# Conditioning weights of a decoder step's first norm, consumed in nine visits instead of one at a time, with seven more slots for weight chunks

## The chip, the cores and the metric

The kernel runs on one core of a Trainium2 chip. The metric is the device time of one execution in microseconds; lower is better. The core's engines work side by side, each in the order of its own instruction stream: TensorE (PE in the profile, with weight loads apart as PEld), VectorE (DVE), ScalarE (ACT), GpSimd (POOL) and SyncE (SP), which here issues the transfers of the weights. Matmuls read SBUF and write PSUM; DVE and ACT empty PSUM.

## The reference

One layer of a hybrid decoder for 256 prompt tokens and 8 x 4 sample tokens, 288 columns in all, model width 2048, in fp32:

```
mod = silu(c) @ w_ada + b_ada            # c: 1 prompt row + 8 sample rows; 6 parts of 2048
sh1, sc1, g1, sh2, sc2, g2 = split(mod, 6)
h = rmsnorm(x, norm1) * (1 + sc1) + sh1
proj = h @ w_in                          # u_pool 512 | z 1536 | xbc 2560 | dt 24
pool_out = pool_mixer(u_pool)            # trailing windows 2, 4, 8, 16
ssd_out = ssd_mixer(z, xbc, dt)          # conv, chunked scan, gated rmsnorm
x = x + g1 * (concat(pool_out, ssd_out) @ w_out)
h2 = rmsnorm(x, norm2) * (1 + sc2) + sh2
x = x + g2 * conv_ffn(h2)                # w_up, causal conv, silu gate, w_down
y = rmsnorm(x, norm_f)
```

The states (pool, conv, ssm, ffn) are outputs too.

## The kernel before

Activations lie with features on the partitions, 16 tiles of 128 features by 288 tokens. Each projection is made of three matmuls in a reduced fp32 format: weights and activations are split into a high and a low part, and `mm3` (L233 to L235) adds high x high, high x low and low x high. Splitting a weight chunk takes one ACT copy (L227) and one DVE subtraction (L228) in `split`.

All weights come as one stream of chunks of up to 128 x 1024 fp32 (512 KB), fetched by `load` on SP's queue into slots. The class `_W` holds the slots, eight for raw chunks (tag `raw`) and two for split ones (tag `wsp`); it goes round them in turn, so a load waits until the chunk in its slot has been used up.

The start of the layer is done in feature groups, `KGROUPS`: (0, 1), (1, 1), (2, 2), (4, 4), (8, 4), (12, 4), first tile and number of tiles. For each group two things are done. First, the shift and scale of its features are computed from `w_ada` ("conditioning", `ada_group_units`): 4, 4, 8, 16, 16, 16 chunks; each chunk's matmuls have the 32 columns of `sc_c` as their stationary operand, so four of them stand side by side in the array (`tile_position`), unsplit fp32, and all add up in one PSUM bank (`adag`). Then ACT copies the result (`asb_g`, L267), PE transposes it (`adat_g`, L273 or L309), DVE adds the bias, and `modulate` (L357 to L369) makes the group's operands `h1k`, high and low. Second, `xbc_units` multiplies the group's tiles with their part of `w_in` for 28 output tiles, called units; a unit has 3, 3, 6, 12, 12, 12 matmuls by group. After each unit its PSUM bank is emptied: copied by ACT in the first group, added by DVE in the later ones (L562) to `cvp`, `upp`, `ups` or `zy`.

The conditioning of the next group is interleaved with the units of the present one:

```
if i >= NX[gi]:
    next(nxt, None)          # one more chunk: matmuls of the last one, load of the next
if i == ET - 4:
    drain(nxt)
    modulate(...)            # operands of the next group
```

The last group has no such work; its loop first makes the dt projection (`mm_dt`) and `dt_stage`, then interleaves the Mamba part and later conditioning (`ada_part_units`, L331). That one already works in visits: four chunks are loaded, and their matmuls run in one piece, the chunk that was loaded last first, the others with high priority and kept in program order.

The program is written with a tile framework. It puts each engine's instructions in order by a model of when they can run, with program order as the priority, and adds the semaphores. A pool is a stretch of SBUF; pool `mx` holds the tiles of the first part of the layer. A tile with a tag shares the tag's slots with others of that tag: the input tiles `xa` and later the recurrent states (`h0`) are `blk`, four slots; the initial conv and pool states (`st`, loaded in `late_loads`, at the fifth group) and later the conv outputs are `cf`.

Of the kernel before, what the change touches and what calls it, by code (L numbers as in the profile page):

```python
# [11 lines left out]
F32 = mybir.dt.float32  # L12
# [5 lines left out]
P = 128  # L18
# [9 lines left out]
NH = 24  # L28
# [10 lines left out]
RAW1, RAW2 = 8, 1  # L39
SPLIT1, SPLIT2 = 2, 2  # L40
PHASE = (192, 32, 0)
YK = 2
NX = (10, 1, 1, 1, 1)
# [89 lines left out]
def kernel(ctx: ExitStack, tc, ins, outs):  # L133
# [148 lines left out]
    def ada_group_units(gi):  # L282

        k0, gk = KGROUPS[gi]
        nj = min(2 * gk, 4)
        nb = 2 * gk * P // nj
        per = RAWC // (nj * nb)
        ps = pa.tile([P, 512], F32, tag="ada", name=f"adag{gi}")
        for q in range(KT // per):
            raw = load(("ada", gi, q))  # L290
            yield
            if gk == 1:

                for kk in range(0, per, 2):
                    k = q * per + kk
                    for j in range(4):
                        nc.tensor.matmul(ps[32 * j:32 * j + 32, :nb], sc_c[:, k + j // 2, :],
                                         raw[:, kk * 256 + j * P:kk * 256 + j * P + P],
                                         start=(k == 0), stop=(k == KT - 2), tile_position=(0, 32 * j))
                if gi == 0 and q < WU[3]:  # L300
                    warm_pe(WU[2], raw[:, 0:P])
                continue
            for kk in range(per):
                ada_mm(ps, raw, q * per + kk, kk * nj * nb, nb, range(nj))
# [67 lines left out]
    class _W:  # L372
# [23 lines left out]
    mx = mx_ctx.enter_context(tc.tile_pool(name="mx", bufs=1))  # L396
    xa = []
# [45 lines left out]
    def late_loads():  # L443
# [3 lines left out]
        st = mx.tile([P, XT * NB * 3 + 4 * NB * 15], F32, tag="cf", name="st", bufs=2)  # L447
# [14 lines left out]
    def dt_stage(ps):  # L462
        tmp = kp.tile([NH, 4, N], F32, tag="hmod", name="dttmp", bufs=2)
        e, z, w, xb = (tmp[:, i, :] for i in range(4))
        t = mx.tile([NH, 2, N], F32, tag="cf", name="dtt", bufs=2)
# [16 lines left out]
        an = mx.tile([NH, 1], F32, name="an")  # L482
# [10 lines left out]
        tok = mx.tile([P, 2, 3, NH], F32, name="tok")  # L493
# [14 lines left out]
        csd = mx.tile([P, 2, 3, NH], F32, name="csd")  # L508
# [9 lines left out]
        ex = mx.tile([P, 2, NH], F32, name="ex")  # L518
# [5 lines left out]
        dm = mx.tile([32, NB, NH], F32, tag="cm", name="dm")  # L524
# [46 lines left out]
    def conv_group(g):  # L571
        cf = mx.tile([P, 5, CW], F32, tag="cf", name=f"cf{g}", bufs=2)
# [14 lines left out]
        ncv = mx.tile([P, 5, 27], F32, tag="ncv", name=f"ncv{g}")  # L587
# [32 lines left out]
    def ssd_group(g):  # L620
# [19 lines left out]
        bt = mx.tile([P, 3, P], F32, tag="bt", name=f"bt{g}")  # L640
# [10 lines left out]
        cb = mx.tile([P, N], F32, tag="cb", name=f"cb{g}")  # L651
# [7 lines left out]
        s1 = mx.tile([P, G6], F32, tag="s1", name=f"s1_{g}")  # L659
# [3 lines left out]
        hf = mx.tile([P, G6], F32, tag="hf", name=f"hf{g}")  # L663
# [5 lines left out]
        s2 = mx.tile([P, G6], F32, tag="s2", name=f"s2_{g}")  # L669
# [4 lines left out]
        cm = mx.tile([P, NB * 36], F32, tag="cm", name=f"cm{g}")  # L674
# [9 lines left out]
        yo = mx.tile([P, G6], F32, tag="yo", name=f"yo{g}")  # L684
# [7 lines left out]
        def decays(t):  # L692

            e = mx.tile([P, 2, N], F32, tag="e", name=f"e{g}_{t}", bufs=2)
            ec = mx.tile([P, 2, P], F32, tag="ec", name=f"ec{g}_{t}", bufs=2)
# [67 lines left out]
    def pool_units(g):  # L763
# [3 lines left out]
        for st in range(g + 1):  # L767
            tp = kp.tile([P, 15 + NP], F32, tag="xsq", name=f"pp{g}_{st}", bufs=2)
            ts_ = mx.tile([P, NB, 19], F32, tag="pools", name=f"pq{g}_{st}", bufs=2)
# [48 lines left out]
    drain(ada_group_units(0))  # L818
    modulate(xav(0, KGROUPS[0][1]), rstd1p, 0, 0, 0, KGROUPS[0][1], "g0")
# [452 lines left out]
```

## Time and profile before

| | us |
|---|---|
| median of 3 runs (lowest, highest) | 1378.83 (1378.32, 1379.18) |
| the profiled execution, its time | 1381.55 |
| the profiled execution, its span | 1379.8 |
| matmul xbc, L233, 448 of them, busy | 139.6 |
| matmul adag, L262, 512 records, busy | 39.9 |
| matmul adap, L331, 288 records up to 420 us, busy | 35.8 |

In a row of the profile, L262 is line 262 of the kernel, `x8` the number of instruction records taken together (a plain fp32 matmul leaves two), and a name such as `adag<-raw_ada,sc_c` says which tile is written from which. Starts and durations are in us from the start of the span. A bracket at the end of a row gives the engine's idle time ahead of it and what ended it. Matmuls are pipelined and their ends modelled, so the distance between starts says more than the duration.

### The profile page before, as it was taken

How to read it: one execution, taken by the hardware profiler on the slowest of the kernel's cores; microseconds unless marked ns; L12 is line 12 of the kernel's file. 1: busy time of each engine (PE TensorE's matmuls, PEld its weight loads, DVE VectorE, ACT ScalarE, POOL GpSimd, SP SyncE). 2: the span in 40 equal slices, each digit the busy share in tenths (PEclk: the TensorE clock that was granted, in tenths of full speed). 3: DMA queues.
4: the chain of work that ended last, by engine and by line, in shares of the span. 5: the costliest groups of instructions: out<-in, count | busy, mean ns of one | idle time of the engine just before them, and what ended most of it. 6: DMA issues, size and time to landing. Idle time of an engine off the chain costs nothing.

```text
span 1379.8 us, 26352 instructions
## 1 busy us (share of the span) xinstructions
PE 1358.6 (98%) x10565; PEld 1246.1 (90%) x10565; DVE 823.6 (60%) x1448; ACT 575.2 (42%) x925; POOL 232.0 (17%) x428
## 2 busy tenths in 40 slices
PE   9999999999999999999999999999999999999997
PEld 7677888777769998999999999999999999999997
DVE  3775657878774347745565445665654556566543
ACT  5222333378754334533443333434433334443452
POOL 0000001122122123211221001221120012132221
PEclk9999999999999999999999999999999999999998
DMA  8889887888878986688655555655555565555531
GB/s 340 308 297 310 306 289 259 303 304 296 329 283 318 354 289 249 215 295 293 209 185 181 172 173 183 200 190 189 179 182 173 177 194 189 196 191 196 183 119 69
DMA packets 97194, 323.20 MB, mean 234 GB/s; under 512 B 10736, under 2 KB 19888, under 8 KB 97072
## 3 DMA queue, kind: packets, MB, share of 16 engines
q1 hardware_dynamic: 93168, 310.63, 65.6%
q0 software_dynamic: 3184, 9.69, 1.9%
q8 instruction: 83, 1.36, 0.4%
q10 hardware_dynamic: 720, 1.19, 0.2%
q14 instruction: 39, 0.32, 0.1%
HBM read 309.78 MB, written 10.39 MB: 232 GB/s over the span
## 4 chain that ended last, share of the span: by engine, by line
PE 93%; DVE 3%; DMA 1%; ACT 1%; issue 1%; POOL 0%; SPq 0%; DVEq 0%; POOLq 0%; ACTq 0%
PE mm_down L234 7%; PE mm_down L235 7%; PE mm_down L233 7%; PE mm_val L234 6%; PE mm_gate L234 6%; PE mm_gate L233 6%; PE mm_val L235 6%; PE mm_gate L235 6%; PE mm_val L233 6%; PE xbc L233 5%; PE xbc L234 4%; PE xbc L235 4%; PE adap L331 4%; PE mm_out L234 3%; PE mm_out L233 3%; PE mm_out L235 2%
## 5 line engine op out<-in xcount | busy, mean ns | idle before, releaser
L234 PE MATMUL mm_down<-ahl,wsp_down 128*128 128x288 f32 x688 | 204.3, 297 | 0.0
L235 PE MATMUL mm_down<-ahl,wsp_down 128*128 128x288 f32 x688 | 202.8, 295 | 0.0
L233 PE MATMUL mm_down<-ahl,wsp_down 128*128 128x288 f32 x688 | 202.1, 294 | 0.0
L234 PE MATMUL mm_val<-h2k,wsp_val 128*128 128x288 f32 x640 | 190.1, 297 | 0.0
L234 PE MATMUL mm_gate<-h2k,wsp_gate 128*128 128x288 f32 x640 | 190.0, 297 | 0.0
L235 PE MATMUL mm_val<-h2k,wsp_val 128*128 128x288 f32 x640 | 188.8, 295 | 0.0
L235 PE MATMUL mm_gate<-h2k,wsp_gate 128*128 128x288 f32 x640 | 188.8, 295 | 0.0
L233 PE MATMUL mm_gate<-h2k,wsp_gate 128*128 128x288 f32 x640 | 188.8, 295 | 0.0
L233 PE MATMUL mm_val<-h2k,wsp_val 128*128 128x288 f32 x640 | 188.0, 294 | 0.0
L228 DVE TENSOR_TENSOR wsp_gate<-raw_gate,wsp_gate 128x1024 fp32r<-128x1024 f32 x80 | 98.0, 1226 | 137.6 <-ACT wsp_gate L227 137.6
L228 DVE TENSOR_TENSOR wsp_down<-raw_down,wsp_down 128x1024 fp32r<-128x1024 f32 x96 | 107.3, 1118 | 121.9 <-ACT wsp_down L227 121.0
L227 ACT CAST wsp_down<-raw_down 128x1024 fp32r<-128x1024 f32 x96 | 92.2, 960 | 167.3 <-PE mm_down L235 116.8
L227 ACT CAST wsp_gate<-raw_gate 128x1024 fp32r<-128x1024 f32 x80 | 83.9, 1050 | 162.2 <-PE mm_gate L235 71.3
L233 PE MATMUL xbc<-h1k,wsp_xbc 128*128 128x288 f32 x448 | 139.6, 313 | 3.5 <-ACT h1k L368 1.7
L227 ACT CAST wsp_val<-raw_val 128x1024 fp32r<-128x1024 f32 x80 | 84.1, 1051 | 119.7 <-issue 98.8
L234 PE MATMUL xbc<-h1k,wsp_xbc 128*128 128x288 f32 x448 | 133.4, 298 | 0.3 <-DVE h1k L369 0.3
L235 PE MATMUL xbc<-h1k,wsp_xbc 128*128 128x288 f32 x448 | 132.6, 298 | 0.1
L233 PEld LDWEIGHTS mm_down<-ahl,wsp_down 128*128 128x128 f32 x688 | 129.6, 188 | 0.0
L234 PEld LDWEIGHTS mm_down<-ahl,wsp_down 128*128 128x128 f32 x688 | 129.3, 188 | 0.0
L235 PEld LDWEIGHTS mm_down<-ahl,wsp_down 128*128 128x128 f32 x688 | 129.2, 188 | 0.0
L233 PEld LDWEIGHTS mm_gate<-h2k,wsp_gate 128*128 128x128 f32 x640 | 120.5, 188 | 5.0 <-ACT ahl L1037 4.2
L233 PEld LDWEIGHTS mm_val<-h2k,wsp_val 128*128 128x128 f32 x640 | 120.6, 188 | 0.0
(318 smaller groups left out, 3013.0 us busy)
## 6 DMA issues: line engine op xcount, KB each, us to landing
raw_adap<-wflat SPq DMA_DIRECT2D x128, 512.0 KB, 5.4
raw_gate<-wflat SPq DMA_DIRECT2D x80, 512.0 KB, 3.5
raw_val<-wflat SPq DMA_DIRECT2D x80, 512.0 KB, 3.6
raw_ada<-wflat SPq DMA_DIRECT2D x64, 512.0 KB, 5.7
raw_xbc<-wflat SPq DMA_DIRECT2D x55, 512.0 KB, 6.0
raw_down<-wflat SPq DMA_DIRECT2D x48, 512.0 KB, 3.6
raw_out<-wflat SPq DMA_DIRECT2D x32, 512.0 KB, 7.4
raw_down<-wflat SPq DMA_DIRECT2D x32, 384.0 KB, 3.0
```

The source lines that it names most:

```text
L227: nc.scalar.copy(hi[:, :n], raw[:, a:a + n])
L228: nc.vector.tensor_tensor(lo[:, :n], raw[:, a:a + n], hi[:, :n].bitcast(F32), ALU.subtract)
L233: nc.tensor.matmul(ps, whi[:, w], bh, start=first, stop=False)
L234: nc.tensor.matmul(ps, whi[:, w], bl, start=False, stop=False)
L235: nc.tensor.matmul(ps, wlo[:, w], bh, start=False, stop=last)
L331: i = nc.tensor.matmul(ps[32 * j:32 * j + 32, :512], sc_c[:, k, :], raw[:, (j % 2) * 512:(j % 2) * 512 + 512], start=(k == ay - 1), stop=( ...
```

## The change

Three things are done.

The conditioning of the groups after the first is consumed in visits. A visit loads four chunks (for the second and third group) or eight (for the fourth to sixth) and then runs their matmuls without a break, in the manner of the later conditioning. `VISIT` gives the size and the units after which a visit stands: after unit 10 of the first group's loop; 7 and 15 of the second's; 8 and 19 of the third's to fifth's. `MOD` gives how many units before the end `modulate` stands: 4, 5, 6, 6, 6.

Seven more raw slots (pool `w0`) are in use from the end of the first group's conditioning until the last group begins. They lie where tiles lie that are needed only from then on: those tiles move from pool `mx` to a pool `m2`, opened when `w0` is closed. `remove` takes the seven slots out of the round.

The tile `st` takes a `blk` slot instead of a `cf` slot.

```diff
+RAW0 = 7
-NX = (10, 1, 1, 1, 1)
+VISIT = {1: (4, (10,)), 2: (4, (7, 15)), 3: (8, (8, 19)), 4: (8, (8, 19)), 5: (8, (8, 19))}
+MOD = (4, 5, 6, 6, 6)
...
-        for q in range(KT // per):
-            raw = load(("ada", gi, q))
-            yield
...
+        n = 0
+        visit = VISIT[gi][0] if gi else 1
+        for v in range(0, nq, visit):
+            raws = [(q, load(("ada", gi, q))) for q in range(v, v + visit)]
+            if not gi:
+                yield
+            begun = False
+            for q, raw in raws[::-1]:
+                for j, k, w in steps(q, raw):
+                    with tc.high_priority() if begun else nullcontext():
+                        i = nc.tensor.matmul(ps[32 * j:32 * j + 32, :nb], sc_c[:, k, :], w, start=n < 4,
+                                             stop=n >= (KT if gk > 1 else KT // 2) * 4 - 4,
+                                             tile_position=(0, 32 * j))
+                    if begun:
+                        tc.keep_in_program_order(i)
+                    begun = gi > 0
+                    n += 1
                 if gi == 0 and q < WU[3]:
                     warm_pe(WU[2], raw[:, 0:P])
...
+            if gi:
+                yield
...
+        def remove(self, pool):
+            for tag, s in self.slots.items():
+                r = self.i[tag] % len(s)
+                self.slots[tag] = [x for x in s[r:] + s[:r] if x[0] is not pool]
+                self.i[tag] = 0
...
-        st = mx.tile([P, XT * NB * 3 + 4 * NB * 15], F32, tag="cf", name="st", bufs=2)
+        st = mx.tile([P, XT * NB * 3 + 4 * NB * 15], F32, tag="blk", name="st", bufs=4)
...
-        t = mx.tile([NH, 2, N], F32, tag="cf", name="dtt", bufs=2)
+        t = m2[0].tile([NH, 2, N], F32, tag="cf", name="dtt", bufs=2)
...
     drain(ada_group_units(0))
+    w0 = w0_ctx.enter_context(tc.tile_pool(name="w0", bufs=1, reuse_waits="tile"))
+    wp[0].add(w0, RAW0, 0)
...
         if last:
+            wp[0].remove(w0)
+            w0_ctx.close()
+            m2[0] = mx_ctx.enter_context(tc.tile_pool(name="m2", bufs=1, reuse_waits="tile"))
...
-                if i >= NX[gi]:
-                    next(nxt, None)
-                if i == ET - 4:
+                if i in VISIT[gi + 1][1]:
+                    next(nxt)
+                if i == ET - MOD[gi]:
                     drain(nxt)
                     modulate(xav(k0, gk), rstd1, 0, 0, k0, gk, f"g{gi + 1}")
```

More of the change, by code (lines that the diff above doesn't have):

```diff
@@ L288, in ada_group_units, with steps @@
         ps = pa.tile([P, 512], F32, tag="ada", name=f"adag{gi}")
-        for q in range(KT // per):
-            raw = load(("ada", gi, q))
-            yield
+        nq = KT // per
+        def steps(q, raw):
             if gk == 1:
                 for kk in range(0, per, 2):
-                    k = q * per + kk
                     for j in range(4):
-                        nc.tensor.matmul(ps[32 * j:32 * j + 32, :nb], sc_c[:, k + j // 2, :],
-                                         raw[:, kk * 256 + j * P:kk * 256 + j * P + P],
-                                         start=(k == 0), stop=(k == KT - 2), tile_position=(0, 32 * j))
+                        yield j, q * per + kk + j // 2, raw[:, kk * 256 + j * P:kk * 256 + j * P + P]
+            else:
+                for kk in range(per):
+                    for j in range(nj):
+                        c = (kk * nj + j) * nb
+                        yield j, q * per + kk, raw[:, c:c + nb]
+        n = 0
[15 more added lines that the diff above has]
+                    n += 1
                 if gi == 0 and q < WU[3]:
                     warm_pe(WU[2], raw[:, 0:P])
-                continue
-            for kk in range(per):
-                ada_mm(ps, raw, q * per + kk, kk * nj * nb, nb, range(nj))
+            if gi:
+                yield
         r = 32 * nj
@@ L396 @@
     mx = mx_ctx.enter_context(tc.tile_pool(name="mx", bufs=1))
+    m2 = [None]
+    w0_ctx = ExitStack()
     xa = []
```

34 lines of the change are left out of this document (17 added, 17 removed).

## The prediction

> **What bounds the kernel now.** I read the page first: span, engine shares, the chain that ended last.
>
> ```profile
> span 1379.8 us, 26352 instructions
> PE 1358.6 (98%) x10565; PEld 1246.1 (90%) x10565; DVE 823.6 (60%) x1448; ACT 575.2 (42%) x925; POOL 232.0 (17%) x428
> PE 93%; DVE 3%; DMA 1%; ACT 1%; issue 1%; POOL 0%; SPq 0%; DVEq 0%; POOLq 0%; ACTq 0%
> ```
>
> PE carries 93% of the chain, so a change pays if it takes time out of PE's own sequence, as long as nothing else becomes late. The change touches only the five feature groups before the last. I located each group in PE's timeline by counting xbc matmuls (28 units, three matmuls for each of 1, 1, 2, 4, 4 feature tiles: 84, 84, 168, 336, 336) and asked the table of windows for these stretches. The last row ends where the dt projection begins. Columns: stretch, length, busy PE, PEld, DVE, ACT, POOL, granted clock, DMA share, GB/s.
>
> ```profile
> 21.80:38.40 16.60, 16.48 (x166) 13.80 (x167) 7.92 (x13) 14.31 (x55) 0.65 (x2) 1.00 0.85 317
> 38.40:64.80 26.40, 24.65 (x239) 16.22 (x237) 17.54 (x58) 5.97 (x10) 1.46 (x2) 1.00 0.86 297
> 64.80:100.20 35.40, 34.59 (x282) 25.92 (x282) 25.98 (x72) 9.37 (x13) 1.69 (x2) 1.00 0.83 305
> 100.20:154.90 54.70, 54.70 (x446) 47.08 (x444) 34.98 (x77) 15.24 (x18) 2.85 (x7) 1.00 0.87 298
> 154.90:212.00 57.10, 57.10 (x470) 47.70 (x469) 32.75 (x75) 15.75 (x19) 0.99 (x2) 1.00 0.88 300
> ```
>
> PE is full in each row, DMA is 83 to 88% busy, and only ACT in the first group and DVE in the second and third come near. What PE's fullness consists of shows in its timeline: a single chunk of conditioning weights, two in one visit, four in one visit (the later, already bundled kind), and a quarter chunk alone.
>
> ```profile
> 159.48 0.29 PE L235 MATMUL xbc<-h1k,wsp_xbc 128*128 128x288 f32 x1
> 159.71 0.64 PE L262 MATMUL adag<-raw_ada,sc_c 128*32 128x256 f32 x8
> 160.28 0.40 PE L233 MATMUL xbc<-h1k,wsp_xbc 128*128 128x288 f32 x1
> 160.51 0.30 PE L234 MATMUL xbc<-h1k,wsp_xbc 128*128 128x288 f32 x1
> 160.65 0.30 PE L235 MATMUL xbc<-h1k,wsp_xbc 128*128 128x288 f32 x1
> ...
> 71.56 0.29 PE L235 MATMUL xbc<-h1k,wsp_xbc 128*128 128x288 f32 x1
> 71.79 1.07 PE L262 MATMUL adag<-raw_ada,sc_c 128*32 128x256 f32 x16
> 72.79 0.40 PE L233 MATMUL xbc<-h1k,wsp_xbc 128*128 128x288 f32 x1
> 73.03 0.29 PE L234 MATMUL xbc<-h1k,wsp_xbc 128*128 128x288 f32 x1
> ...
> 256.32 0.29 PE L235 MATMUL xbc<-h1k,wsp_xbc 128*128 128x288 f32 x1
> 256.55 1.92 PE L331 MATMUL adap<-raw_adap,sc_c 128*32 128x512 f32 x16
> 258.64 0.29 PE L234 MATMUL xbc<-h1k,wsp_xbc 128*128 128x288 f32 x1
> ...
> 52.33 0.29 PE L235 MATMUL xbc<-h1k,wsp_xbc 128*128 128x288 f32 x1
> 52.55 0.62 PE L262 MATMUL adag<-raw_ada,sc_c 128*32 128x256 f32 x2
> 53.34 0.29 PE L234 MATMUL xbc<-h1k,wsp_xbc 128*128 128x288 f32 x1
> ```
>
> Starts are read, since ends are modelled. Two xbc matmuls in sequence start 0.13 us apart (160.51, 160.65). Each excerpt holds three xbc matmuls, two steps or 0.26 us, and the rest is the visit. One chunk: 160.51 - 159.48 - 0.26 = 0.77 us. Two chunks: 73.03 - 71.56 - 0.26 = 1.21. Four: 258.64 - 256.32 - 0.26 = 2.06. So a visit costs 0.33 us for entering and leaving and 0.43 to 0.44 us for each chunk; 0.33 + 4 x 0.43 = 2.05 agrees with the four. A quarter chunk alone costs 0.75 where 0.33 + 0.11 would be its share, 0.3 more.
>
> The visits that this change regroups run from the first to the last of these rows, 64 in count (6, 16, 13, 13, 16 by row of the window table):
>
> ```profile
> 23.30 0.41 PE L297 MATMUL adag<-raw_ada,sc_c 128*32 128x128 f32 x2
> ...
> 195.07 0.64 PE L262 MATMUL adag<-raw_ada,sc_c 128*32 128x256 f32 x8
> ```
>
> **The change part by part.**
>
> *Visits.* 60 chunks (4, 8, 16, 16, 16) are now fetched in 9 visits: one of four, two of four, six of eight. The matmuls stay the same in number and form. 55 crossings fewer at 0.33 us are 18.2 us; some 13 visits of a part of a chunk, at about 0.3, are 4 more. PE alone would gain 22 us. It doesn't get all, by group:
>
> First group: ACT evacuates its PSUM, and PE waited on it where it was not in a visit.
>
> ```profile
> L560 ACT COPY cvp<-xbc 128x256 f32<-128x256 f32 x20 | 7.4, 378 | 1.8 <-PE xbc L235 1.8
> 51.13 0.37 PE L233 MATMUL xbc<-h1k,wsp_xbc 128*128 128x288 f32 x1 [1.12 <-DVE cvp L562]
> ```
>
> ACT is busy 14.31 of 16.60 us and idle 1.8 ahead of its main copies: what PE saves, it waits for ACT. Gain 0 (bounds 0 and 1.8).
>
> Second and third group, taken together since chunks move between them: 61.8 us before. PE after: 252 xbc matmuls x 0.1315 = 33.1, two visits of four (4.1) and two of eight (2 x 3.77 = 7.5): 44.8 us. DVE's work is unchanged, 17.54 + 25.98 = 43.5 us. Two engines equally full do not fit perfectly into each other; the row at 51.13 shows PE held 1.12 us by DVE's evacuation already. And a cover goes: the handover to the next group's operands is a chain of copies, transposes and DVE work:
>
> ```profile
> 88.04 0.37 ACT L267 COPY asb_g<-adag 128x256 f32<-128x256 f32 x1 [5.19 <-PE adag L262]
> 98.17 1.55 DVE L369 TENSOR_TENSOR h1k<-h_g,h1k 128x288 fp32r<-128x288 f32 x4
> 98.79 1.50 PE L262 MATMUL adag<-raw_ada,sc_c 128*32 128x256 f32 x22
> 100.24 0.38 PE L233 MATMUL xbc<-h1k,wsp_xbc 128*128 128x288 f32 x1
> ```
>
> From the copy to the last operand it took 11.7 us (88.04 to 99.72), covered by units of the old group and, at 98.79, by visits for a later one. After, the last visit stands behind unit 19; 8 units of 6 matmuls, 8 x 6 x 0.1315 = 6.3 us, are left as cover, and no small visit is at hand. I charge 3 us for this handover, 2 for the second group's (12 units of 3 matmuls, 4.7 us, as cover, for a chain half as wide) and 2 for evacuation: 52 us. Gain 9.8; bounds 44.8 and 58 (17.0 and 3.8), the latter with 3 us more at each handover.
>
> Fourth group: 336 x 0.1315 = 44.2, plus 2 x 3.77: 51.7 us for 54.7, gain 3.0. Fifth: 51.7 plus 0.5 for transposes against 57.1, gain 4.9. Here 8 units leave 12.6 us of cover for the 11.7 us chain, and DVE is busy 35 of 55 us.
>
> *Seven slots and the loads.* The bytes stay. All loads go in SP's order; a visit's eight loads stand ahead of the next xbc chunks' loads there, and its first matmul waits for the last of them; behind it waits all of PE. Over the five rows the DMA moved 317 x 16.6 + 297 x 26.4 + 305 x 35.4 + 298 x 54.7 + 300 x 57.1, in total 57.3 MB in 190.2 us, 301 GB/s at a share of 0.86, so about 350 GB/s at full share. The new length, 190.2 - 17.7 = 172.5 us, needs 332. With a deep queue more has been seen:
>
> ```profile
> 20.00:25.00 5.00, 3.73 (x26) 3.12 (x26) 3.56 (x5) 3.25 (x12) 1.23 (x2) 1.00 1.03 407
> 140.00:145.00 5.00, 5.00 (x40) 5.00 (x40) 4.54 (x14) 2.38 (x5) 2.85 (x7) 1.00 1.03 415
> 240.00:245.00 5.00, 5.00 (x27) 3.80 (x27) 3.71 (x12) 1.50 (x4) 1.44 (x4) 0.76 0.80 323
> 245.00:250.00 5.00, 5.00 (x25) 1.88 (x23) 2.31 (x4) 2.81 (x6) 0.04 (x1) 0.55 0.05 6
> ```
>
> Fifteen slots (7.9 MB) allow such a queue where eight could not. I charge 1.5 us of waits at the first visits of eight; bounds 0 and 10.
>
> *Moved tiles.* The state load takes a slot of the input tiles, free since the third group's operands were made; the first recurrent-state loads move one slot on, and their readers come only in the last group: 0. The later tiles open in w0's place once its last chunks are split, ahead of the dt stage: 0. Weight loads of the last group have eight slots as before: 0.
>
> Sum: 0 + 9.8 + 3.0 + 4.9 - 1.5 = 16.2 us. The profiled execution took 1381.55 us (span 1379.8 and 1.75 around it); after, 1365.3. The median 1378.83 stands 2.7 below the profiled time, so the forecast for the median is **1362.6 us**. What follows the groups is unchanged and should only begin earlier.
>
> **The rivals.**
>
> *A: PE gets everything.* Handovers and evacuation hide: second and third group 45 us, no DMA wait. Gain 17 + 3 + 4.9 = 24.9, some 1354 us. Against it: DVE at 43.5 of 45 and the row at 51.13. The Trainium skill's page "DMA: Bandwidth & Descriptors", Specifications, gives about 358 GB/s as HBM's limit per core; the two groups load 18.1 MB, which by that would take 50.5 us and leave A no better than 1360. The rows with 407 and 415 GB/s speak against the limit here, in stretches of 5 us only.
>
> *B: the loads bind.* If the mean rate stays at 301 GB/s, 57.3 MB take the same 190 us, PE saves crossings and waits for loads instead: 1378, no change. For it: DMA shares of 0.83 to 0.88. Against: the 407 and 415. Halfway, at 315 GB/s, 182 us: 1371.
>
> *C: the visits don't come out whole.* If the compiler's order splits them as it split the chunk at 52.55, crossings remain: 1377. Against it the row at 256.55, made by the same construction, 16 records in one piece.
>
> *D, the slower one: the half clock.* The rows from 240 to 250 us show the clock at 0.76 and 0.55 while PE did little but small matmuls. If each of the six visits of eight (or the wait before it) is taken for such a stretch and costs as much as that one did (0.24 + 0.45 of 5 us, 3.45 us), it is 20.7 us, against 16.2 gained: 1383. It decides from 2.7 us for each of the six. Against it: from 15 to 20 us PE ran nothing but fp32 matmuls of the small kinds, and the clock stayed at 1.00.
>
> ```profile
> 15.00:20.00 5.00, 4.62 (x73) 3.91 (x73) 1.56 (x6) 1.61 (x3) 0.25 (x1) 1.00 1.03 406
> ```
>
> The Trainium skill, "TensorE: Matmul & The Clock Gate", Part 1, says that the gate halves the clock after an idle window of about 3.4 us. By that rule a visit alone, which keeps PE busy, costs nothing, and only waits of that length would; the trace shows none so long in the five groups, yet shows the drop at 245 with PE marked busy.
>
> **How the numbers follow.** The forecast's own case (gain 9 to 21, 1358 to 1370) has 0.62; A 0.14; partial B (1370 to 1376) 0.12; full B and C, no change, 0.07; D 0.05. The range 1355 to 1374 leaves out D, full B, C and the tails, about 2 in 10. A difference under 0.2% (2.8 us) cannot be told from none: faster 0.88, same 0.07, slower 0.05.
>
> **What will show it.** Right: 9 pieces of adag after 21 us, each of 64 records, about 3.6 us from the start of an eight to the next xbc (1.85 for a four); the fifth group's stretch near 52 us; some idle before the third and fourth groups' first xbc, ended by h1k; dt projection starting near 195 us instead of 212; GB/s above 330 in the five rows. Wrong: PE idle ahead of adag ended by raw_ada loads, clock below 1.00 around the visits, many pieces, or a later stage (last group, uz) that grows by what the groups gave.

## The result, and the profile after

The changed kernel took 1370.39 us (median of 4 runs, 1368.8 to 1371.33) beside 1379.01 us of the kernel before (4 runs on the same chip, 1378.32 to 1381.14): a ratio of 0.9934 with a 95% interval of 0.9917 to 0.9951. The forecast for the median was 1362.6, so 8.6 us came where 16.4 were expected. The profiled execution took 1371.33 us (span 1369.5), 10.2 us less than that of before; the two traces are compared below.

First the page of the changed kernel, the lines that answer to those of before.

```profile
span 1369.5 us, 26363 instructions
PE 1338.9 (98%) x10565; PEld 1249.5 (91%) x10565; DVE 826.8 (60%) x1448; ACT 575.3 (42%) x925; POOL 230.4 (17%) x428
PE 90%; DMA 4%; DVE 3%; ACT 1%; issue 0%; POOL 0%; SPq 0%; DVEq 0%; POOLq 0%; ACTq 0%
```

PE is busy for 19.7 us less (1358.6 before), with the same 10565 matmuls, but the span fell by only 10.3. The rest is time in which PE stands still. The table of windows shows in which stretch, cut again from one group's first xbc matmul to the next, the last row up to the dt projection (columns as before: stretch, length, PE, PEld, DVE, ACT, POOL, clock, DMA share, GB/s).

```profile
21.80:37.30 15.50, 14.97 (x151) 13.50 (x151) 7.88 (x13) 14.27 (x55) 0.65 (x2) 1.00 1.03 408
37.30:56.80 19.50, 16.91 (x215) 15.15 (x213) 17.01 (x57) 6.00 (x9) 0.62 (x2) 1.00 1.03 407
56.80:94.00 37.20, 33.22 (x298) 28.81 (x299) 27.71 (x74) 8.63 (x12) 0.94 (x2) 0.93 0.83 312
94.00:148.30 54.30, 52.88 (x468) 49.12 (x468) 33.71 (x76) 16.40 (x19) 2.53 (x7) 0.99 0.87 334
148.30:202.30 54.00, 54.00 (x485) 48.81 (x484) 32.81 (x75) 15.86 (x19) 1.07 (x3) 1.00 0.78 276
```

The lengths were 16.6, 26.4, 35.4, 54.7 and 57.1 us, and are 15.5, 19.5, 37.2, 54.3 and 54.0. The last row now holds a visit that before lay behind the dt projection, the 16 adap matmuls at 197.15 us, which take 2.1 us; without it the fifth group has 51.9.

PE's timeline shows each visit in a single piece, one of eight for example:

```profile
67.02 0.29 PE L237 MATMUL xbc<-h1k,wsp_xbc 128*128 128x288 f32 x1
67.24 3.66 PE L314 MATMUL adag<-raw_ada,sc_c 128*32 128x256 f32 x64
70.83 0.40 PE L235 MATMUL xbc<-h1k,wsp_xbc 128*128 128x288 f32 x1
```

Less one step of 0.13 us between two xbc matmuls, the visit of eight costs 70.83 - 67.02 - 0.13 = 3.68 us and one of four, at 46.72, 1.98. By start times over the five groups, PE spends 22.6 us less in visits and in the slower steps around them.

What was given back is seen in PE's waits over the five groups, the largest, first of the kernel before, then of the changed one (columns: who waits, for whom, us in total, times, longest):

```profile
PE xbc L233 <- ACT h1k L368: 1.7, 2, 1.3
PE xbc L233 <- DVE cvp L562: 1.7, 3, 1.1
```

```profile
PE xbc L235 <- DVE zy L590: 4.0, 2, 2.6
PE xbc L235 <- ACT h1k L388: 3.4, 2, 2.1
PE xbc L235 <- DVE cvp L590: 1.0, 3, 0.4
```

The largest is new: PE waits for VectorE's additions of z tiles (L590), which empty PSUM. Where two xbc matmuls start 0.3 us and more apart, what exceeds the step of 0.13 us is a gap; the gaps grew from 2.4 to 11.0 us in all. The large ones lie where one group hands over to the next (given as distances of starts): 2.40 us at 54.4 and 1.31 at 56.8 at the handover to the third group, 2.85 at 89.6 to the fourth, 1.71 at 143.3 to the fifth. Behind the first two handovers the clock is halved for 3.41 us, from 57.9 and from 92.1; the windows:

```profile
55.00:60.00 5.00, 2.29 (x9) 2.07 (x10) 5.00 (x11) 1.64 (x3) 0.62 (x2) 0.79 1.03 410
90.00:95.00 5.00, 2.58 (x11) 2.58 (x12) 4.36 (x10) 1.46 (x3) 0.00 (x0) 0.71 1.03 419
```

In both windows VectorE is nearly or wholly full while PE is half empty. What it does at 88 to 94 us is in its timeline:

```profile
87.91 0.83 DVE L380 TENSOR_SCALAR h_g<-h_g,amul,ada 128x256 f32<-128x256 f32 x2
88.66 1.21 DVE L230 TENSOR_TENSOR wsp_xbc<-raw_xbc,wsp_xbc 128x1024 fp32r<-128x1024 f32 x1
89.80 0.72 DVE L380 TENSOR_SCALAR h_g<-h_g,amul,ada 128x256 f32<-128x256 f32 x2
90.45 1.55 DVE L389 TENSOR_TENSOR h1k<-h_g,h1k 128x288 fp32r<-128x288 f32 x4
91.92 1.17 DVE L590 TENSOR_TENSOR zy<-zy,xbc 128x288 f32<-128x288 f32 x3
```

PE's side of it:

```profile
89.57 0.29 PE L237 MATMUL xbc<-h1k,wsp_xbc 128*128 128x288 f32 x1
92.42 0.61 PE L235 MATMUL xbc<-h1k,wsp_xbc 128*128 128x288 f32 x1 [2.56 <-DVE zy L590]
```

From 87.91 to 91.92 VectorE makes the next group's operands (L380 scales, L389 low parts, a split of weights between) and three evacuations of the old group stand behind that in its queue. PE has more of the old group's matmuls to do, but no PSUM bank to put them in until the first evacuation ends: that is the wait of 2.56 us. The Trainium skill, "TensorE: Matmul & The Clock Gate", section "Architectural detail: the array is 16× 32×32, not 1× 128×128", says that VectorE and ScalarE take their queue strictly in order; the trace agrees with that here, as the z additions at 91.92 started behind steps that PE didn't wait for, although the last matmul of their units had started at 89.57.

In the kernel before, VectorE's order at this handover was another:

```profile
94.53 0.40 DVE L360 TENSOR_SCALAR h_g<-h_g,amul,ada 128x256 f32<-128x256 f32 x1
94.97 0.45 DVE L562 TENSOR_TENSOR zy<-zy,xbc 128x288 f32<-128x288 f32 x1
95.34 0.73 DVE L360 TENSOR_SCALAR h_g<-h_g,amul,ada 128x256 f32<-128x256 f32 x2
95.99 0.45 DVE L562 TENSOR_TENSOR zy<-zy,xbc 128x288 f32<-128x288 f32 x1
96.35 0.41 DVE L360 TENSOR_SCALAR h_g<-h_g,amul,ada 128x256 f32<-128x256 f32 x1
96.67 0.45 DVE L562 TENSOR_TENSOR zy<-zy,xbc 128x288 f32<-128x288 f32 x1
```

The scales alternate with the z additions. Only the split and the low parts, from 97.04 to 99.72, stand together, and the visit at 98.79, which needs nothing from VectorE, covers their end. So two things changed at this place: VectorE's operand steps stand in one block, and no visit stands beside them. The order is the framework's; why it came out so, no run shows.

So the reading of the two traces is: 22.6 us taken out, 8.6 us given back as gaps, and 2.5 us more in steps stretched by the halved clock; 11.5 us net in the groups, of which 9.6 show at the start of the last group (208.6 against 218.1); the rest is the adap visit of 2.1 us. What made the gaps, and whether the clock or the slots mattered, is what the runs below decide.

### The profile page after: what moved, and what is told of

Its sections match the earlier page's. It is cut to its first block, busy times and chain, and to the rows that moved or that the text cites. A ratio compares the mean times of both kernels' runs of the same rounds, so it can differ in the third digit from the quotient of the medians.

```text
span 1369.5 us, 26363 instructions
## 1 busy us (share of the span) xinstructions
PE 1338.9 (98%) x10565; PEld 1249.5 (91%) x10565; DVE 826.8 (60%) x1448; ACT 575.3 (42%) x925; POOL 230.4 (17%) x428
## 4 chain that ended last, share of the span: by engine, by line
PE 90%; DMA 4%; DVE 3%; ACT 1%; issue 0%; POOL 0%; SPq 0%; DVEq 0%; POOLq 0%; ACTq 0%
PE mm_down L236 7%; PE mm_down L237 7%; PE mm_down L235 7%; PE mm_val L236 6%; PE mm_gate L236 6%; PE mm_gate L235 6%; PE mm_gate L237 6%; PE mm_val L237 6%; PE mm_val L235 6%; PE xbc L235 4%; PE adap L351 4%; PE xbc L236 4%; PE xbc L237 4%; PE mm_out L235 3%; PE mm_out L236 2%; PE mm_out L237 2%
## 5 line engine op out<-in xcount | busy, mean ns | idle before, releaser
L230 DVE TENSOR_TENSOR wsp_down<-raw_down,wsp_down 128x1024 fp32r<-128x1024 f32 x96 | 108.0, 1125 | 121.8 <-ACT wsp_down L229 121.8
L230 DVE TENSOR_TENSOR wsp_gate<-raw_gate,wsp_gate 128x1024 fp32r<-128x1024 f32 x80 | 98.1, 1228 | 136.2 <-ACT wsp_gate L229 136.1
```

Of the source, the lines that this page charges most:

```text
L230: nc.vector.tensor_tensor(lo[:, :n], raw[:, a:a + n], hi[:, :n].bitcast(F32), ALU.subtract)
```

## The experiments

All ratios are against the kernel before, with 95% intervals. The changed kernel's own is 0.9934 [0.9917, 0.9951].

The runs act on the five groups alone, but what follows the groups also differs from trace to trace. So this table, worked out from the profiled execution of each, separates the two. "Groups" goes from the first xbc matmul to the dt projection, without the adap visit where it lies ahead of it; "rest" goes on to the end of the span, with that visit added, so that it holds the same work in all.

| | median time, us | groups, us | rest, us |
|---|---|---|---|
| before | 1379.01 | 190.0 | 1167.9 |
| changed kernel | 1370.39 | 178.4 | 1169.3 |
| `slots` | 1380.57 | 190.0 | 1169.2 |
| `noslots` | 1387.55 | 195.7 | 1165.9 |
| `early` | 1370.48 | 178.3 | 1167.6 |
| `warm` | 1371.03 | 178.5 | 1171.1 |
| `lessdve` | 1372.97 | 176.2 | 1172.8 |
| `mod` | 1370.74 | 180.9 | 1165.8 |
| `earlymod` | 1373.63 | 182.5 | 1168.8 |
| `split3` | 1370.34 | 178.0 | 1167.4 |
| `acts` | 1363.69 | 173.8 | 1166.6 |
| `cover` | 1367.03 | 174.5 | 1170.3 |
| `poollow` | 1371.91 | 179.8 | 1170.4 |
| `actsprio` | 1363.07 | 173.6 | 1166.5 |

The rest varies by 7 us, and no run explains it. A difference of a few microseconds in the time alone therefore says little about a handover; the groups say more.

### Which half of the change does what: slots alone, visits alone

`slots` keeps single chunks as before (NX in place of VISIT, operand steps at ET - 4) and takes the seven slots and the moved tiles.

```
-VISIT = {1: (4, (10,)), 2: (4, (7, 15)), ...}
+NX = (10, 1, 1, 1, 1)
...
-                if i in VISIT[gi + 1][1]:
-                    next(nxt)
-                if i == ET - MOD[gi]:
+                if i >= NX[gi]:
+                    next(nxt, None)
+                if i == ET - 4:
```

> The seven slots and the moved tiles alone; the conditioning chunk by chunk as before the change. Theory H: the crossings remain (over 55 visits), and so does the time of before, 1377 to 1380 us. Theory L (before, the loads already held PE back): some of the gain comes from the slots, 1371 to 1375 us.

Measured: 1380.57 us, 1.0001 [0.999, 1.0012]. Its windows:

```profile
21.80:38.40 16.60, 16.32 (x165) 13.64 (x166) 7.78 (x13) 14.32 (x56) 0.65 (x2) 1.00 1.03 407
38.40:64.80 26.40, 24.80 (x240) 16.36 (x238) 17.56 (x58) 5.84 (x9) 1.45 (x2) 1.00 0.92 362
```

The DMA moved 407 and 362 GB/s in place of 317 and 297, and PE's stretches are the same to a tenth of a microsecond. The kernel before was not waiting for loads, and the slots alone give nothing.

`noslots` is the converse: the visits, with the eight slots of before.

```
-RAW0 = 7
+RAW0 = 0
```

> The visits alone, with the eight slots of before. Theory H: crossings are saved as in the changed kernel, 22 us, but a visit of eight needs every slot, so its loads go out only as the split chunks leave, 4.2 MB at 0.41 MB/us is 10 us, and behind it no chunk is at hand; six of them cost 4 to 8 us each, 1382 to 1406 us. Rival: the slots are not needed, 1369 to 1373 us.

Measured: 1387.55 us, 1.0047 [1.0031, 1.0064]: slower than before. Two of PE's waits over the groups:

```profile
PE xbc L235 <- ACT wsp_xbc L229: 7.2, 5, 2.1
...
PE adag L314 <- DMA raw_ada<-wflat: 3.2, 2, 3.0
```

Both lines are new: a visit of eight fills all eight slots, the weights of the following xbc chunks come late, and ScalarE's copy of them, for which PE waits, with them. The two visits of the third group take 14.6 us, from the last xbc matmul ahead to the first behind, against 7.6 in the changed kernel. So the visits carry the gain, and the slots make them possible.

### Is the cover too short? Visits earlier

If the gaps came from the last visit standing too near the group's end, moving it forward would close them.

```
-VISIT = {1: (4, (10,)), 2: (4, (7, 15)), 3: (8, (8, 19)), 4: (8, (8, 19)), 5: (8, (8, 19))}
+VISIT = {1: (4, (10,)), 2: (4, (4, 11)), 3: (8, (5, 15)), 4: (8, (7, 17)), 5: (8, (8, 19))}
```

> Visits in the second group's loop after units 4 and 11 instead of 7 and 15, in the third's after 5 and 15 instead of 8 and 19, in the fourth's after 7 and 17 instead of 8 and 19; all else as in the changed kernel (1370.4 us). Theory H (what is missing went into the handovers: PE idles 2.4 + 1.3, 2.85 and 1.7 us there, and the clock is halved after two of them): the chain to the next operands starts 3 to 4 units sooner, 4 to 6 us of the idle time and the 2.5 us of half clock go, 1363 to 1366 us. Theory L (the loads bind): the eight are wanted sooner than they can land, PE waits ahead of adag, 1370 to 1375 us.

Measured: 1370.48 us, 0.9922 [0.9907, 0.9937]. The gaps stayed: 2.40 us at 55.6, 1.31 at 58.0, 2.17 at 91.4, 1.71 at 143.3. That theory falls: ahead of the fourth group ScalarE's copy of the conditioning (L269) ran at 81.54 us, 2.4 us sooner than in the changed kernel, but its transposition stands at 87.10, where `MOD` puts it, and what came behind it was late all the same. PE does not wait ahead of adag either, so the loads are not the reason.

### Does the halved clock cost anything? PE kept warm

Eight 128x128 fp32 matmuls, whose result is not used, are put at the end of the second and third groups' loops to keep PE busy in the gaps.

```
+        if gi in (1, 2):
+            wt = aux(f"fill{gi}")
+            for _ in range(8):
+                tc.keep_in_program_order(nc.tensor.matmul(wt[:, :P], ones, ones, start=True, stop=True))
```

> Eight unused fp32 matmuls (1.7 us) on PE between the last unit of the second group and the first of the third, and the same between third and fourth, where PE idles anyway. Theory H with the clock as a term of its own: the two windows at half clock at 58 and 92 us go, 2.5 us less than the changed kernel, 1367 to 1369 us. Rival: the windows are not brought by the idle time, they stay, and the time is 1370 to 1372 us.

Measured: 1371.03 us, 0.9924 [0.9906, 0.9942], and the same two windows:

```profile
55.00:60.00 5.00, 3.74 (x29) 3.33 (x28) 5.00 (x11) 1.51 (x3) 0.62 (x2) 1.00 1.03 410
90.00:95.00 5.00, 3.54 (x29) 3.54 (x30) 4.73 (x9) 1.09 (x2) 0.00 (x0) 1.00 1.03 414
```

The clock is 1.00 in both, and the groups are as long as in the changed kernel, 19.5 and 37.4 us. Neither forecast had that. That does not show that the halved clock is free; PE's timeline tells where the unused matmuls stand:

```profile
54.40 1.95 PE L917 MATMUL fill<-ones 128*128 128x128 f32 x16
...
92.36 1.95 PE L917 MATMUL fill<-ones 128*128 128x128 f32 x16
```

The first eight fill the gap at 54.4, and the third group's matmuls behind them run 0.8 us ahead of the changed kernel's, counted from the group's first. The second eight stand behind the gap, which is there as before (2.81 us at 88.65), where PE has work again, and their 1.7 us take that gain back. At this second gap the run is no test.

### Is VectorE's total the bound? Less work for it

The 44 additions of sample columns (128x32) of the second and third groups are left out; the sample columns of these tiles are therefore incomplete.

```
+                if gi in (1, 2) and len(parts) == 2:
+                    parts = parts[:1]
```

> The changed kernel without the additions of the 32 sample columns (0.18 us each) after 22 units of the second and 22 of the third group; the sample columns are thus wrong from there on. Theory W (DVE's work in these two groups is what PE idles for: 17.0 of 19.5 us busy in the second): 8 us less DVE work, 3 to 6 us of the idle time goes, 1364 to 1367 us. Theory Q (only the place of the handover's steps in DVE's order counts): each step still stands behind the same evacuations and splits, which are a little shorter, 1368 to 1370 us.

Measured: 1372.97 us, 0.994 [0.9921, 0.996], above both forecasts. PE's largest wait, for VectorE's z additions (L592), is 3.9 us, the changed kernel's 4.0 to a tenth, and the gaps are the same: 2.41 us at 54.4, 1.31 at 56.8, 2.81 at 88.6, 1.71 at 141.2. Work taken from VectorE elsewhere in the loop does not shorten the wait at the handover.

The groups are 2.3 us shorter all the same (the rest is longer, and the time shows nothing of it). Of these, 1.4 us lie behind the gap at 88.6, which is as long as in the changed kernel but is not followed by a halved clock:

```profile
90.00:95.00 5.00, 3.62 (x27) 3.62 (x28) 4.72 (x9) 1.05 (x1) 0.00 (x0) 1.00 1.03 410
```

So of the 2.5 us of stretched steps in the changed kernel some 2.2 were paid in the length of the groups: 1.4 here, and the 0.8 that `warm` saves at the first place.

### Another place for the operand steps

`mod` makes each group's operands earlier in the loop before, `earlymod` does so with the visits of `early`.

```
-MOD = (4, 5, 6, 6, 6)
+MOD = (4, 11, 8, 8, 8)
```

> The changed kernel with the handover (bias, operands) placed 11, 8, 8, 8 units ahead of the end instead of 5, 6, 6, 6, thus sooner in DVE's order; visits where they were. Theory Q: the idle times at the handovers (2.4 + 1.3, 2.85, 1.7 us) shrink by 4 to 6 us, 1364 to 1367 us. Theory W: the steps come sooner, the evacuations later, the idle time moves to waits for PSUM, 1369 to 1372 us, only the fourth group's 1.7 us, where DVE is busy 34 of 54 us, goes.

Measured: 1370.74 us, 0.9927 [0.991, 0.9945]. PE's waits over the groups:

```profile
PE xbc L235 <- DVE cvp L590: 3.7, 4, 1.7
PE xbc L235 <- DVE zy L590: 3.5, 3, 1.8
PE xbc L235 <- DVE ups L590: 2.6, 2, 1.3
```

The wait for operands (h1k) fell from 3.4 to 1.3 us, and those for evacuations (cvp, zy, ups) rose from 5.0 to 9.8. The idle time moved with the operand steps: 1.97 us at 52.5, 2.06 at 91.3, 1.59 at 141.8, and a new 1.59 at 195.2. The groups are 2.4 us longer than in the changed kernel; the equal time comes from the rest.

```
+VISIT = {1: (4, (10,)), 2: (4, (4, 11)), 3: (8, (5, 15)), 4: (8, (7, 17)), 5: (8, (8, 19))}
+MOD = (4, 12, 10, 9, 6)
```

> The earlier visits of the run before (after units 4 and 11, 5 and 15, 7 and 17) and the handover 12, 10, 9 and 6 units ahead of the end. Theory Q: all handovers find their operands ready, 7 to 9 us of idle time go, 1361 to 1364 us. Theory W: third and fourth group gain 2 to 4 us since the third has DVE to spare (27.7 of 37.2 us), the second gains nothing, 1366 to 1369 us.

Measured: 1373.63 us, 0.9953 [0.9938, 0.9968], above both forecasts, with groups 4.1 us longer than the changed kernel's and 3.43 us of idle time in one place at 86.2. In neither of the two placements tried was there room for four microseconds of VectorE ahead of evacuations.

### Is it the slot for split weights?

The split of the next group's first weights needs one of two split slots, and PE frees it late. `split3` gives a third and takes one of the seven raw slots for it.

```
-RAW0 = 7
+RAW0 = 6
...
-    wp[0].add(w0, RAW0, 0)
+    wp[0].add(w0, RAW0, 1)
```

> The changed kernel with six raw slots and one slot more for split chunks (three instead of two) in the place of the seven. Theory W: DVE can split one chunk more during a visit, when it idles now (1.8 us in the third group's second visit), 1367 to 1369 us. Theory Q: nothing, 1370 to 1372 us. If one raw slot more matters, it shows as PE waiting ahead of adag.

Measured: 1370.34 us, 0.9931 [0.9913, 0.9949]; gaps of 2.41 us at 55.6, 1.31 at 58.0, 1.92 at 91.4, 1.72 at 142.7, and a new one of 1.23 at 51.0. The split slot isn't it.

### The burst itself: shorter, covered, shared

The theory left was that the operand steps stand as a burst in VectorE's queue ahead of evacuations, and that PE has nothing to do in it that needs no VectorE. Three runs act on the burst itself. `acts` lets ScalarE do the scale and shift (L380) of the third to the last groups:

```
+            if which == 0 and k0 >= 2:
+                nc.scalar.activation(h[:, i, 0:NP], h[:, i, 0:NP], AF.Identity,
+                                     bias=ada[:, shp, k0 + i, 0:1], scale=amul[:, which, k0 + i, 0:1])
+                continue
             nc.vector.tensor_scalar(h[:, i, 0:NP], h[:, i, 0:NP], amul[:, which, k0 + i, 0:1],
```

> The scale and shift of the 256 prefix columns in the operand steps of the third to last groups (two, four, four and four tiles) run on ScalarE as an activation with scale and bias, in place of VectorE; nothing is left out. Theory B (burst on VectorE): the burst is shorter by 0.8 us at the third group's handover and by 1.5 us at the fourth's and fifth's (0.41 us each), so the gaps there, 2.40 and 1.31, 2.85, 1.71 us, shrink by 0.5, 1.4 and 1.4 us: 1367 to 1368. Rival C (the length of the chain scale, copy, low part sets the gap, on whichever engine): ScalarE has to do scale and copy one behind the other, the gaps stay or grow by 0.4 us each, 1370 to 1372. Rival M (idle time only moves): 1370 to 1371.

Measured: 1363.69 us (6 runs, 1361.32 to 1367.74), 0.9881 [0.9863, 0.9899]: 6.7 us below the changed kernel, and the two intervals don't touch. VectorE's timeline at the same handover:

```profile
88.17 1.22 DVE L230 TENSOR_TENSOR wsp_xbc<-raw_xbc,wsp_xbc 128x1024 fp32r<-128x1024 f32 x1
89.31 1.31 DVE L594 TENSOR_TENSOR zy<-zy,xbc 128x288 f32<-128x288 f32 x3
90.53 0.45 DVE L393 TENSOR_TENSOR h1k<-h_g,h1k 128x288 fp32r<-128x288 f32 x1
```

The z additions that were held until 91.92 now run at 89.31, ahead of the low parts. The gap of 2.85 us is 0.59, and those of 1.31 at the third group's first units and of 1.71 ahead of the fifth group are gone. ScalarE's line in the groups of the trace (columns: duration ns lowest/median/highest, first and last start):

```profile
L381 ACT ACTIVATE h_g<-h_g,ada,amul x14: 586/589/603, 55.5 to 191.5; 128x256 f32<-128x256 f32 x14
```

It takes longer than VectorE's 0.41 us each, but ScalarE has room for it: it is busy for 9.25 and 19.13 us in the two rows below. The Trainium skill, "ScalarE: Activation LUTs", section "What ACT_TABLE_LOAD costs", gives 186 ns, 93 ns more for each pointer operand, and 0.833 ns an element; for 256 elements with scale and bias by pointer that is an estimate of 585 ns. The trace agrees with 589.

The gain was larger than the 1367 to 1368 that the theory had foreseen. In the groups it is 4.6 us (178.4 to 173.8): I had taken only the removed 0.41 us pieces off the gaps, but VectorE's order changed with them, and the evacuations went ahead of the low parts too. So the run doesn't separate the shorter burst from the better order. The other 2.7 us between the two traces lie in the rest, where the edit changes nothing, and are not explained. The windows of the third and fourth group in `acts`:

```profile
57.00:90.40 33.40, 32.53 (x298) 28.10 (x298) 23.08 (x64) 9.25 (x14) 0.83 (x2) 0.95 0.81 308
90.40:143.50 53.10, 52.74 (x467) 48.65 (x468) 33.98 (x75) 19.13 (x26) 3.26 (x7) 1.00 0.90 350
```

They went from 37.2 to 33.4 us and from 54.3 to 53.1; the second group's stretch is 19.8 us in place of 19.5.

`cover` leaves VectorE's work alone and gives PE something to do in the burst: the first visit for the group after next is issued right behind the operand steps.

```
                     modulate(xav(k0, gk), rstd1, 0, 0, k0, gk, f"g{gi + 1}")
+                    if gi in (2, 3):
+                        ahead = ada_group_units(gi + 2)
+                        next(ahead)
```

> The first visit of eight for the fifth group (and for the last) is issued right behind the operand steps of the fourth (fifth) group, at the handover, and only the second visit stays inside the loop that follows; nothing is left out. In the changed kernel TensorE idles 2.85 us at 89.6 and 1.71 us at 143.3, while VectorE works off the burst of operand steps in order and the evacuations stand behind it. Theory B (the idle time is a burst on VectorE, four scales of 0.41 and four low parts of 0.45 us and a split of 1.2, under which TensorE has nothing to do that needs no VectorE): a visit of eight, 3.6 us of TensorE that asks nothing of VectorE, stands in that place; both gaps go to under 0.6 us and the time falls by 3 to 4.5 us, to 1366 to 1367.5. Rival M (idle time only moves, as VectorE's total in the loop sets the pace): the gaps come back elsewhere in the same loops, sum of idle time unchanged, 1370 to 1371. Rival L (the sixteen chunks that are wanted earlier aren't there, as the queue moves 312 to 334 GB/s there): TensorE waits for raw_ada at the visit, up to 10 us for 4 MB, 1372 to 1380.

Measured: 1367.03 us (6 runs, 1363.73 to 1370.9), 0.9904 [0.9887, 0.9921]. Its interval overlaps with the changed kernel's, so the 3.4 us alone would be weak; in the groups it is 3.9 us, and the trace shows the mechanism. PE's timeline:

```profile
87.22 0.29 PE L238 MATMUL xbc<-h1k,wsp_xbc 128*128 128x288 f32 x1
88.10 3.66 PE L315 MATMUL adag<-raw_ada,sc_c 128*32 128x256 f32 x64 [0.58 <-DMA raw_ada<-wflat]
91.69 0.40 PE L236 MATMUL xbc<-h1k,wsp_xbc 128*128 128x288 f32 x1
...
93.46 0.40 PE L238 MATMUL xbc<-h1k,wsp_xbc 128*128 128x288 f32 x1 [1.24 <-DVE wsp_xbc L231]
```

The visit fills the time in which PE waited for z, and no wait for z is left in the five groups; 0.58 us for the loads and 1.24 for a split of weights came in place of 2.85. At the fourth group's end the 1.71 us are gone altogether.

`poollow` puts every second low part on GpSimd.

```
-            nc.vector.tensor_tensor(xlo[0][k0 + i], h[:, i, :], xhi[0][k0 + i].bitcast(F32), ALU.subtract)
+            eng = nc.gpsimd if which == 0 and k0 >= 2 and i % 2 else nc.vector
+            eng.tensor_tensor(xlo[0][k0 + i], h[:, i, :], xhi[0][k0 + i].bitcast(F32), ALU.subtract)
```

> Every second low part in the operand steps of the third to last groups (one, two, two and two tiles) is made on GpSimd in place of VectorE; nothing is left out. Theory B (burst on VectorE): 0.45 us less of the burst at the third group's handover, 0.9 us at the fourth's and fifth's; 2 us in all if GpSimd's own time is covered: 1368 to 1369.5. Rival C (chain): the low part on GpSimd takes longer than 0.45 us (a 128x128 multiplication takes up to 0.58 there), so the second feature tile's third matmul waits for it and the time rises by 0.5 to 1 us at each handover: 1371 to 1374.

Measured: 1371.91 us, 0.9936 [0.9921, 0.9952]. The time lies in the range of rival C. The gaps were 2.42, 1.31, 2.72 and 1.07 us: the last one shrank by 0.64, the others hardly. GpSimd took 1.11 and 0.84 us where VectorE takes 0.45. Beside `acts`, it is also the weaker way to shorten the burst: these low parts come late in it, behind scales and split. As a gain, nothing.

### The last gap: place in the queue

In `acts` 2.74 us are left at 54.2, ahead of the third group, where PE waits for the operand. The bias addition of the conditioning had stood behind evacuations there. `actsprio` gives it and the scaling step priority.

```
+            with tc.high_priority():
                 nc.vector.tensor_tensor(o, src, b.unsqueeze(3).to_broadcast([P, 2, nj // 2, NC9]), ALU.add)
-        ada_scale(0, 1, early[:, V_N1:V_N1 + KT], k0, gk)
+        with tc.high_priority():
+            ada_scale(0, 1, early[:, V_N1:V_N1 + KT], k0, gk)
```

> As the run acts (scale and shift of the operand steps on ScalarE), and in addition the bias addition and the scaling step of each group's conditioning have priority, so that in VectorE's fixed order they stand up to sixteen evacuations earlier, right behind the transposition they need; nothing is left out. In acts the transposition of the third group's conditioning ends at 49.6 us, the bias addition starts at 53.26 and the scaling step at 55.12, behind evacuations and the split of the next weights, and TensorE idles 2.74 us until the operand's copy ends at 56.97. Theory Q (place in VectorE's order): the chain starts 3 to 5 us earlier, the third group's gap goes to under 0.8 us, 2 to 2.5 us are gained there and 0.5 to 1 at the second group: 1360.5 to 1361.5. Rival M (the idle time moves: the addition waits for the transposition with evacuations behind it, so TensorE waits for PSUM at 49 to 51 us instead, as when the steps were put seven chunks earlier): the gap at 49.7 us grows from 0.73 by 1 to 2 us, 1363 to 1365. Rival R (the copy of the next group's weights waits for a split slot and stands ahead of the operand's copy on ScalarE, so the operand comes no earlier): gap at 54 unchanged at 2.4 to 2.8, 1363.5.

Measured: 1363.07 us (4 runs, 1361.86 to 1363.65), 0.9876 [0.9859, 0.9892], not to be told from `acts`. PE's waits:

```profile
PE xbc L235 <- DVE zy L596: 1.9, 1, 1.9
PE xbc L235 <- DVE cvp L596: 1.6, 3, 1.1
PE xbc L235 <- ACT h1k L394: 1.5, 2, 1.3
```

The largest wait for the operand is gone and two for evacuations took its place (1.39 us of gap at 49.8, 2.21 at 54.5). Here the rival that the idle time only moves was right. The second group's stretch holds 17.0 to 17.6 us of VectorE's work in 19.5 to 20.7, and PE's idle time there was moved by `mod` and `actsprio` and removed by no run.

At this handover one more thing stands in VectorE's way, in the changed kernel:

```profile
53.05 1.05 ACT L229 CAST wsp_xbc<-raw_xbc 128x1024 fp32r<-128x1024 f32 x1 [4.05 <-DMA raw_ada<-wflat]
```

ScalarE's copy of weights had waited 4.05 us for a load, with the DMA share at 1.03 over the whole group. The split that needs the copy (L230, 54.13 to 55.36) stands in VectorE's queue ahead of the scaling step (L279) at 55.27. So the loads may own a part of the 2.40 us; no run separates it.

## Why the prediction was right, and where it was off

The direction held, and so did the mechanism of the gain: fewer crossings. The size was half of what was forecast. 1370.39 us lies in the range of 1355 to 1374, at the very end of the forecast's own case (1358 to 1370). Rival A, everything for PE at 1354, fell. By the prediction's steps:

*Visits.* A crossing of 0.33 us and 0.43 a chunk gave 3.77 us for an eight and 2.05 for a four; taken in the same way, to the second xbc matmul behind the visit less two steps, 3.79 (71.07 - 67.02 - 0.26) and 2.09 were measured. The 22 us that PE alone would gain were 22.6. Rival C (visits don't come out whole) fell: each is one piece of 64 records.

*First group.* Gain 0 within 0 and 1.8: 1.1 measured.

*Second and third group.* 52 us forecast, with 7 us charged on PE's 44.8; 56.7 measured (19.5 + 37.2). PE's gaps in the two were 3.07 + 5.29 = 8.4 us, near the charge; transposes and odd steps, which my 44.8 left out, were 1.9, and stretched steps 1.8. The term was short by 4.7 us, within its bounds of 44.8 and 58. That the 7 us charged came near these 8.4 is in part luck. At the handover to the third group PE waited for the operands (h1k), as put. At the handover to the fourth it waited for z additions (2.56 us), not for operands as put: the cover of old units was counted as free (8 x 6 x 0.1315 us), although each of those units needs VectorE for its evacuation, and VectorE was busy with the operands. With `acts` 3.8 us of the third group's 37.2 went.

*Fourth group.* This is the step that failed outright: gain 3.0 forecast, 0.4 measured (54.3 for 54.7). I charged nothing, since "8 units leave 12.6 us of cover for the 11.7 us chain, and DVE is busy 35 of 55 us". The share over the group said nothing of the four microseconds at its end: the gap of 1.71 us at 143.3 is the same burst, and `acts` and `cover` both remove it. The other 0.9 us is steps stretched by the halved clock at its start and odd ones.

*Fifth group.* Gain 4.9 forecast, 5.2 measured, once the adap visit is set apart. Its operands belong to the last group, and no gap was there.

*Loads.* I charged 1.5 us of waits; PE never waited ahead of adag. That the loads cost nothing is not shown: the copy that waited 4.05 us until 53.05 stands in the chain that leads to the operands of the third group. For the time as a whole rival B fell, since the first two rows ran at 408 and 407 GB/s. The sign of more than 330 GB/s held in three rows and failed in two (312 and 276); the mean over the five is 326. `slots` shows 407 and 362 GB/s in the first two rows with no change in time. The limit of about 358 GB/s per core, which the prediction took from the Trainium skill's "DMA: Bandwidth & Descriptors", Specifications, and which that page gives further down as a core's share with both cores of a pair streaming, did not hold here with one core running: 407 to 408 GB/s held over the first two rows, 35 us.

*Moved tiles.* 0, as `slots` at 1.0001 confirms for the tiles and slots together.

*Rival D, the half clock.* The visits did not bring it: the clock is 1.00 in the second and 0.99 or more in the fourth and fifth rows. Two of the waits did, with 3.41 us each at 57.9 and 92.1, and it cost about 2.2 us (see `warm` and `lessdve`), for which the prediction's own case had no term.

Sum of the groups: 1.1 + 5.1 + 0.4 + 5.2 = 11.8 us where 0 + 9.8 + 3.0 + 4.9 - 1.5 = 16.2 stood (11.6 in the table, as the last row of before ends at 212.0 and the dt projection begins at 211.84). The dt projection began at 202.3 us, not near 195, of which the adap visit is 2.1. Of the 11.6 us, 1.4 were lost again in the rest. That leaves the 10.2 us by which the profiled executions differ; the medians differ by 8.6, since the profiled execution of before lay 2.5 us above its median and that of the changed kernel 0.9. In `acts` the dt projection begins at 195.4, and its groups, 173.8 us, are what the forecast gave (190.2 - 16.2 = 174.0): what it took for granted, that the operand steps of the fourth and fifth groups are hidden, is nearly what that edit makes true.

Open is what comes after the groups. From the last group's first xbc matmul to the end it took 1161.7 us before, 1160.9 in the changed kernel and 1160.3 in `acts`, although only the changed kernel has the adap visit already behind it. The difference arises ahead of the w_out projection, whose first matmul comes 183.2, 183.7 and 180.8 us after that xbc matmul. Halved clock falls in different places there (3.41 us each at 378.8 and 395.9 in the changed kernel, once at 389.0 in `acts`); whether that accounts for it was not tried.

## What to carry to other kernels

Putting filler work together saves its crossings, but it also changes what stands beside what, and in which order. Here the kernel before had VectorE's operand steps between evacuations and beside small visits; the changed one had them in one block, with no visit beside it. Before grouping such filler, look at each place where an in-order engine gets several microseconds of work at once, and ask which evacuations stand behind it; an average share of 60 or 70% busy doesn't answer that. Where a burst is uncovered, the two other places tried for it only moved the idle time or lengthened it. Giving part of it to an engine with room took 4.6 us off the groups, and keeping one piece of the filler for that place 3.9.

## What the runs showed of the hardware that I had not expected

- One core's loads ran at 407 GB/s over 35 us at a stretch with a queue of fifteen buffers of 512 KB, at a DMA share of 1.03, and 419 in a 5 us window, where the kernel before had means of 297 to 317 over its five groups.
- A stand of 2.1 us and another of 0.9 us right behind it were followed by a halved clock: granted clock 0.79 over 55 to 60 us. At the handover to the fourth group one of 2.56 us was (0.71 over 90 to 95), but in `lessdve` one of 2.52 us at the same place was not (1.00 over 90 to 95). So the length of a stand alone doesn't decide it. The Trainium skill, "TensorE: Matmul & The Clock Gate", Part 1, speaks of a whole idle window of about 3.4 us; here PE was not idle that long without a break.
- ScalarE's scale and shift of 128x256 took 0.589 us against VectorE's 0.41, and was the cheaper place all the same: the groups became 4.6 us shorter.
